# Low parts of the channel MLPs' second weights: a DMA adds the block to its negated high part, in place of a subtraction on VectorE

## The chip, the cores and the metric

One core of one Trainium2 chip. The metric is device time in microseconds: two runs of the kernel before took 1291.55 and 1291.85 us, median 1291.7.

## The reference

Two layers, each a token mixer followed by a channel MLP, on 512 tokens of width 1024. What matters here is the channel MLP, with 4096 hidden features:

```
for i in range(DEPTH):
    ...
    h = rmsnorm(x, norm_g[i, 2]) * (1.0 + sc2) + sh2
    y = jnp.square(jax.nn.relu(h @ ffn_w1[i])) @ ffn_w2[i]
    x = x + g2 * rmsnorm(y, norm_g[i, 3])
```

ffn_w2[i] is 4096 x 1024 in float32. Everything is float32.

## The kernel before

All large products are float32 products made of three products in float32r: each operand is split into a high part, which is its rounding to float32r, and a low part, the difference. mm3 issues high x high, then high x low, then low x high, where the activations are the stationary operand in the second product of the MLP and the weights the moving one.

A channel MLP (ffn) runs in two halves of 2048 hidden features. In a half, the first projection makes 16 tiles of hidden features: TensorE fills a PSUM bank, ScalarE applies relu into a tile t, POOL squares it, ScalarE rounds it to the high part, VectorE subtracts to the low part (tiles a). Then the second product runs over two column blocks of 512 outputs (cb) and two groups of eight K-chunks (k0): w_rows loads four K-chunks by 512 columns as one raw tile of 1 MB, and conv splits it in two blocks [128, 2, 512]; two calls make the four blocks of a group. In a group, four token tiles t follow one another, and each goes through all four blocks: 24 products per token tile, 96 per group, 6 per token tile and block. So there are four groups in a half and 16 such groups in the kernel.

conv makes the high part whi on ScalarE (a cast) and the low part wlo on VectorE (a subtraction). Both come from the pool wp with four buffers each, shared with all other weights; raw tiles come from rp with three buffers, all loads on SP's queue. While the last token tile of a group runs, TensorE releases a block's two buffers after the sixth product on it, and the next group's block is formed into them.

After the first part of the mLSTM mixer the order on each engine is not the order of the code: a scheduler sets it from its own costs (pinned is False from there on), and each engine runs its own list in order. In the lists below a name's last number tells tiles apart.

Of the kernel before, what the change touches and what calls it, by code (L numbers as in the profile page):

```python
# [8 lines left out]
F32 = mybir.dt.float32  # L9
F32R = mybir.dt.float32r  # L10
# [5 lines left out]
P = 128  # L16
# [17 lines left out]
def trunk(ctx: ExitStack, tc: tile.TileContext, x, c, norm_g, ada_w, ada_b, ffn_w1, ffn_w2,  # L34
# [5 lines left out]
    class Engine:  # L40
        """an engine whose instructions keep their traced order while `pinned` is set."""

# [56 lines left out]

# [1 line left out]
    ident = cp.tile([P, P], F32, name="ident")  # L101
# [19 lines left out]

    # silu of the conditioning vector, one column per K-chunk
    ck = cp.tile([8, P], F32, name="ck")
# [8 lines left out]

    # per-feature columns: norm_g (64), hnorm_g (8), b_b_in first half (16); ada_b (96)
    pk = A()[:, 0:2 * P].rearrange("p (a b) -> p a b", a=2)
# [16 lines left out]

# [1 line left out]
    def ada_load(l, vs, vc, k):  # L153
# [37 lines left out]
    def ada_ab(l, vs, vc, ng, k):  # L191
        """scale/shift columns for feature chunk k: h = A * xn + B."""
        raw = ada_load(l, vs, vc, k)
        acc = R().rearrange("p (c i f) -> p c (i f)", c=2, i=2)
        ada_init(raw, acc)
        ada_acc(raw, acc, range(6))
        return ada_fin(ada_tr(acc), l, vs, vc, ng, k)

    def ada_g(box, l, v, ng):
        """gate * norm gain, broadcast over partitions: [P, D]."""  # L200
        g = gp.tile([P, D], F32, tag="g", name=nm("g"))
        box.g = g
        w = ada_w[l].rearrange("(k p) f -> p k f", p=P)
        for s in range(2):
            f0 = v * D + s * S
            acc = R()
            pool.memset(acc, 0.0)
            ld.dma_start(acc[0:1, :], ada_b[l:l + 1, f0:f0 + S])
            for hf in range(2):
                raw = rp.tile([P, 4, S], F32, tag="raw", name=nm("raw"))  # L210
                ld.dma_start(raw, w[:, hf * 4:hf * 4 + 4, f0:f0 + S])
                for j in range(4):
                    kk = hf * 4 + j
                    dve.scalar_tensor_tensor(out=acc, in0=raw[:, j], scalar=cact[:, kk:kk + 1],
                                             in1=acc, op0=ALU.mult, op1=ALU.add)
                yield
            ngb = R()
            ld.dma_start(ngb, norm_g[l, ng:ng + 1, s * S:(s + 1) * S].broadcast_to([P, S]))
            ps = bank3()
            hi, lo = T(F32R), T(F32R)  # L220
            act.copy(hi, acc)
            dve.tensor_sub(lo, acc, f32(hi))
            pe.matmul(ps, lhsT=ones, rhs=hi, start=True, stop=False)
            pe.matmul(ps, lhsT=ones, rhs=lo, start=False, stop=True)
            dve.tensor_mul(g[:, s * S:(s + 1) * S], ps, ngb)
            yield

# [1 line left out]
    def conv(raw_ap, scale=None, lo_eng=None):  # L229
        """exact split of a weight block (optionally with its rows scaled) into two float32r parts."""  # L230
        shp = list(raw_ap.shape)
        hi = wp.tile(shp, F32R, tag="whi", name=nm("whi"))
        lo = wp.tile(shp, F32R, tag="wlo", name=nm("wlo"))
        if scale is None:
            act.copy(hi, raw_ap)
            (lo_eng or dve).tensor_sub(lo, raw_ap, f32(hi))
        else:
            for i, c in enumerate(scale):
                act.activation(hi[:, i], raw_ap[:, i], AF.Copy, scale=c)
                dve.scalar_tensor_tensor(out=lo[:, i], in0=raw_ap[:, i], scalar=c, in1=f32(hi[:, i]),  # L240
                                         op0=ALU.mult, op1=ALU.subtract)
        return hi, lo

    def w_cols(w, f0):
        """two blocks [P, KC, 128] of 128 output features each."""
        raw = rp.tile([P, KC, 2 * P], F32, tag="raw", name=nm("raw"))
        ld.dma_start(raw, w[:, f0:f0 + 2 * P].rearrange("(k p) f -> p k f", p=P))
        return [conv(raw[:, :, i * P:(i + 1) * P]) for i in range(2)]

    def w_rows(w, k0, f0, scale=None):  # L250
        """four K-chunks x 512 output features, as two blocks [P, 2, 512]."""
        raw = rp.tile([P, 4, S], F32, tag="raw", name=nm("raw"))
        ld.dma_start(raw, w[k0 * P:(k0 + 4) * P, f0:f0 + S].rearrange("(k p) f -> p k f", p=P))
        return [conv(raw[:, 2 * i:2 * i + 2], scale and scale[k0 + 2 * i:k0 + 2 * i + 2]) for i in range(2)]
# [5 lines left out]

    # At the end of a sub-layer the first transposes of token tile t are queued behind the product
    # of K-chunk j of a unit u; units 0..3 are the last token tiles, 4.. the next sub-layer's first.
    places = {0: (2, 1), 1: (3, 1), 2: (4, 6), 3: (6, 2)}
    held = {}

    def behind(ins, later):
        """queue ins behind a later traced product."""
        nosync = mybir.DependencyInfo(mybir.DependencyClass.NoSync, mybir.DependencyReason.DATA)
        tc.add_manual_dep(ins.ins, later.ins.name, nosync, reason="issue order")

    class HT:
        """normalised, modulated activations: [feature, token], split."""

# [23 lines left out]

# [1 line left out]
    def rstd_of(parts):  # L299
        """(sum of parts + eps) ** -0.5, parts already hold means."""  # L300
        v = small(1)
        if len(parts) == 2:
            dve.tensor_scalar(v, parts[0], parts[1], EPS, ALU.add, ALU.add)
        else:
            dve.tensor_scalar_add(v, parts[0], EPS)
        r = small(1)
        pool.tensor_tensor(out=r, in0=v, in1=mhalf[:, 0:1], op=ALU.pow)
        return r
# [35 lines left out]
    def residual(t, yg, mss):  # L344
        """x += yg * rstd, yg = gate * norm gain * y in two halves."""
        r = rstd_of(mss)
# [4 lines left out]
    def out_proj(w, h, prep, nk, after, scale=None):  # L351
        """y = h @ w (token major), x += g * rmsnorm(y); after(t) follows each token tile."""
        y = [[None] * 2 for _ in range(NT)]
# [19 lines left out]

# [1 line left out]
    def ffn(l, h, prep, after):  # L375
# [3 lines left out]
        for half in range(2):  # L379
# [37 lines left out]
            for cb in range(2):  # L417
                banks = [bank() for _ in range(NT)]
                for k0 in range(0, 16, 8):
                    blks = w_rows(w2, half * 16 + k0, cb * S) + w_rows(w2, half * 16 + k0 + 4, cb * S)  # L420
                    for t in range(NT):
# [13 lines left out]

# [1 line left out]
    def mlstm(h, prep, after):  # L437
# [3 lines left out]
        for t in range(NT):  # L441
            xx = xp.tile([P, D], F32, tag="x", name=f"x{t}")
            ld.dma_start(xx, x[0, t * P:(t + 1) * P, :])
            xt.append(xx)
        # gate weights, padded with zero columns
        wgs = w.rearrange("(k p) f -> p k f", p=P)
# [107 lines left out]
        qT, kT = [], []  # L554
        # gates: rows 0..7 input gate, 32..39 forget gate
        gt = A()
# [24 lines left out]

        # k
        for f0 in (512, 768):
# [6 lines left out]

        # cumulative log forget gate per chunk, heads on partitions
        ps = bank2()
# [61 lines left out]
        def decay(n):  # L654
            """exp(u_j - m_i), zero for j > i; heads of one parity to a tile."""
            dec.append([])
# [10 lines left out]

        # v, token major with a column of ones per head; three heads to a tile
        vt = [[A(shape=(P, 3, DV + 1)) for _ in range(3)] for _ in range(NT)]
# [31 lines left out]

        # output gate
        so = [[None] * 2 for _ in range(NT)]
# [34 lines left out]
        def mixed(n):  # L738
            ts = slice(n * P, (n + 1) * P)
            pr = dec[n]  # L740
            # columns of the small tiles: e * 4 + p for head 2 * p + e
            ex = scv[:, n, 64:72].rearrange("p (a e) -> p e a", e=2)
# [92 lines left out]

# [1 line left out]
    def sgu(h, prep, after):  # L837
# [8 lines left out]
        def ln_cols():  # L846
            """layer norm gain and bias as feature columns."""
            pk = A()[0:2 * NG, 0:P]
# [6 lines left out]
        def mix_weights(q):  # L855
            """causal spatial weights of four groups, transposed, and their row sums."""
            ws = A()
# [22 lines left out]
        def offsets(q):  # L880
            """what the mix adds to u's factor besides gain * mixed: bias * row sum + bs."""
            rb = A()
# [97 lines left out]

# [1 line left out]
    def store(t):  # L982
# [3 lines left out]
    class Prep:  # L986
        """gate of this sub-layer and scale/shift of the next, in steps run among other work."""

# [63 lines left out]
```

## Time and profile before

| | |
|---|---|
| timed runs, median | 1291.7 us (1291.55 to 1291.85) |
| profiled execution, first to last instruction | 1288.8 us |
| TensorE busy | 1241.9 us |
| VectorE busy | 679.2 us |
| ScalarE busy | 523.9 us |
| POOL busy | 240.0 us |
| read from HBM | 171.11 MB |

The profile is of one execution. The timed runs hold what lies before the first and after the last instruction as well, 2.9 us at the median. PE is TensorE, DVE VectorE, ACT ScalarE, SPq and POOLq the queues of SyncE and GpSimd that issue DMAs. Nearly every instruction carries line 50, that of the helper which records it, so instructions are told apart by the tiles they write and read: wlo<-raw,whi is the subtraction of conv, ps<-wlo,a a product of the second MLP projection with a low part of the weights.

### The profile page before, as it was taken

How to read it: one execution, taken by the hardware profiler on the slowest of the kernel's cores; microseconds unless marked ns; L12 is line 12 of the kernel's file. 1: busy time of each engine (PE TensorE's matmuls, PEld its weight loads, DVE VectorE, ACT ScalarE, POOL GpSimd, SP SyncE). 2: the span in 40 equal slices, each digit the busy share in tenths (PEclk: the TensorE clock that was granted, in tenths of full speed). 3: DMA queues.
4: the chain of work that ended last, by engine and by line, in shares of the span. 5: the costliest groups of instructions: out<-in, count | busy, mean ns of one | idle time of the engine just before them, and what ended most of it. 6: DMA issues, size and time to landing. Idle time of an engine off the chain costs nothing. (4 is left out here: it accounts for less than half of the span.)

```text
span 1288.8 us, 15198 instructions
## 1 busy us (share of the span) xinstructions
PE 1241.9 (96%) x5849; PEld 1019.1 (79%) x5849; DVE 679.2 (53%) x1124; ACT 523.9 (41%) x923; POOL 240.0 (19%) x230
## 2 busy tenths in 40 slices
PE   3999899999999999999999999999999999999997
PEld 2677777888778888888778888888887888888886
DVE  6897666576863343323786766623566222333225
ACT  4535534384433244413563644323653321343221
POOL 5602311013320022200120023200132200122000
PEclk9999999999999999999999999999999999999999
DMA  9756842425762443222367555322255214322201
GB/s 278 225 186 188 256 125 75 137 74 163 214 212 98 132 138 98 98 98 74 130 200 255 158 153 146 109 101 69 95 165 171 98 66 131 99 98 98 98 33 66
DMA packets 165610, 174.25 MB, mean 135 GB/s; under 512 B 6168, under 2 KB 120936, under 8 KB 165536
## 3 DMA queue, kind: packets, MB, share of 16 engines
q1 hardware_dynamic: 165408, 173.17, 42.5%
q8 instruction: 46, 0.75, 0.2%
q14 instruction: 28, 0.23, 0.1%
q0 software_dynamic: 128, 0.09, 0.0%
HBM read 171.11 MB, written 2.14 MB: 134 GB/s over the span
## 5 line engine op out<-in xcount | busy, mean ns | idle before, releaser
L50 PE MATMUL ps<-whi,a 128*128 128x512 f32 x1408 | 437.1, 390 | 0.0
L50 DVE TENSOR_TENSOR wlo<-raw,whi 128x1024 fp32r<-128x1024 f32 x196 | 241.4, 1236 | 313.8 <-ACT whi L50 304.0
L50 ACT CAST whi<-raw 128x1024 fp32r<-128x1024 f32 x196 | 205.0, 1050 | 287.0 <-PE ps L50 252.1
L50 PEld LDWEIGHTS ps<-whi,a 128*128 128x128 f32 x1408 | 264.3, 188 | 54.5
L50 PE MATMUL ps<-hlo,whi 128*128 128x512 f32 (+1 forms) x744 | 277.3, 373 | 2.9 <-POOL hlo L50 2.9
L50 PE MATMUL ps<-hhi,whi 128*128 128x512 f32 (+1 forms) x744 | 279.1, 375 | 0.5 <-ACT whi L50 0.5
L50 PE MATMUL ps<-hhi,wlo 128*128 128x512 f32 (+1 forms) x744 | 277.2, 373 | 0.7 <-DVE wlo L50 0.7
L50 PE MATMUL ps<-wlo,a 128*128 128x512 f32 x704 | 274.4, 390 | 1.0 <-DVE wlo L50 1.0
L50 PEld LDWEIGHTS ps<-hlo,whi 128*128 128x128 f32 x744 | 140.3, 189 | 28.3 <-POOL hlo L50 4.2
L50 DVE SCALAR_TENSOR_TENSOR r<-raw,cact,r 128x256 f32<-128x256 f32 (+1 forms) x256 | 149.3, 622 | 23.8 <-ACT r L50 16.6
L50 PEld LDWEIGHTS ps<-hhi,wlo 128*128 128x128 f32 x744 | 140.2, 188 | 25.6 <-DVE wlo L50 1.5
L50 PEld LDWEIGHTS ps<-hhi,whi 128*128 128x128 f32 x744 | 140.3, 189 | 24.4 <-ACT whi L50 0.9
L50 POOL TENSOR_TENSOR t<-t 128x512 f32<-128x512 f32 x64 | 98.4, 1537 | 314.9 <-ACT t L50 314.9
L50 PEld LDWEIGHTS ps<-wlo,a 128*128 128x128 f32 x704 | 132.2, 188 | 28.9 <-DVE wlo L50 1.9
L50 POOL TENSOR_TENSOR s<-s,mhalf 128x1 f32<-128x1 f32 (+1 forms) x40 | 33.9, 847 | 378.8 <-DVE s L50 371.4
L50 PE MATMUL ps<-whi,hhi 128*128 128x512 f32 x256 | 101.6, 398 | 1.4 <-ACT whi L50 1.3
L50 PE MATMUL ps<-wlo,hhi 128*128 128x512 f32 x256 | 100.5, 393 | 2.4 <-DVE wlo L50 2.4
L50 PE MATMUL ps<-whi,hlo 128*128 128x512 f32 x256 | 100.2, 392 | 0.0
L50 DVE TENSOR_TENSOR a<-t,a 128x512 fp32r<-128x512 f32 x64 | 44.3, 692 | 77.2 <-ACT a L50 75.8
L50 ACT CAST a<-t 128x512 fp32r<-128x512 f32 x64 | 39.7, 621 | 103.3 <-POOL t L50 103.3
L50 POOL TENSOR_TENSOR r<-r 128x256 f32<-128x256 f32 x32 | 32.9, 1028 | 185.4 <-DVE r L50 159.4
L50 PEld LDWEIGHTS ps<-wlo,hhi 128*128 128x128 f32 x256 | 48.1, 188 | 14.4 <-DVE wlo L50 5.1
(128 smaller groups left out, 996.7 us busy)
## 6 DMA issues: line engine op xcount, KB each, us to landing
raw<-in_ffn_w SPq DMA_DIRECT2D x64, 1024.0 KB, 5.3
raw<-in_ada_w SPq DMA_DIRECT2D x64, 512.0 KB, 5.6
raw<-in_ada_w SPq DMA_DIRECT2D x16, 1024.0 KB, 5.0
raw<-in_b_w_in SPq DMA_DIRECT2D x16, 1024.0 KB, 5.5
raw<-in_a_w_in SPq DMA_DIRECT2D x10, 1024.0 KB, 5.1
raw<-in_b_w_out SPq DMA_DIRECT2D x8, 1024.0 KB, 6.3
raw<-in_a_w_out SPq DMA_DIRECT2D x4, 1024.0 KB, 5.0
x<-in_x SPq DMA_DIRECT2D x4, 512.0 KB, 7.6
```

Of the source, the lines that this page charges most:

```text
L50: r = f(*a, **k)
```

## The change

In the second product of the channel MLPs w_rows_acc stands in place of w_rows. ScalarE writes the negated block, rounded to float32r, into lo; a DMA issued by POOL reads the same block from HBM a second time and adds it onto lo; ScalarE casts the block to hi as before. VectorE has no part in it. The other weights keep conv. Lines that only drop a comment are left out.

```diff
@@ -242,13 +242,29 @@
+    def w_rows_acc(w, k0, f0):
+
+
+        raw = rp.tile([P, 4, S], F32, tag="raw", name=nm("raw"))
+        src = w[k0 * P:(k0 + 4) * P, f0:f0 + S].rearrange("(k p) f -> p k f", p=P)
+        ld.dma_start(raw, src)
+        out = []
+        for i in range(2):
+            hi = wp.tile([P, 2, S], F32R, tag="whi", name=nm("whi"))
+            lo = wp.tile([P, 2, S], F32R, tag="wlo", name=nm("wlo"))
+            act.activation(lo, raw[:, 2 * i:2 * i + 2], AF.Copy, scale=-1.0)
+            pool.dma_start(lo, src[:, 2 * i:2 * i + 2], accum_op=ALU.add)
+            act.copy(hi, raw[:, 2 * i:2 * i + 2])
+            out.append((hi, lo))
+        return out
+
@@ -417,7 +433,7 @@
-                    blks = w_rows(w2, half * 16 + k0, cb * S) + w_rows(w2, half * 16 + k0 + 4, cb * S)
+                    blks = w_rows_acc(w2, half * 16 + k0, cb * S) + w_rows_acc(w2, half * 16 + k0 + 4, cb * S)
```

The scheduler orders the engines anew around it. On TensorE, the start of the fourth group of the first half in layer 0; a is a tile of hidden features, ps the bank of a token tile (3694 is the first). Before:

```order
L50 MATMUL ps_3694<-whi_3816,a_3044 128x512
L50 MATMUL ps_3694<-wlo_3817,a_3044 128x512
L50 MATMUL ps_3694<-whi_3816,a_3045 128x512
L50 MATMUL ps_3694<-whi_3816,a_3082 128x512
L50 MATMUL ps_3694<-wlo_3817,a_3082 128x512
L50 MATMUL ps_3694<-whi_3816,a_3083 128x512
L50 MATMUL ps_3694<-whi_3820,a_3134 128x512
L50 MATMUL ps_3694<-wlo_3821,a_3134 128x512
```

The same place now, where 3702 is the bank of the first token tile and 3703 that of the second:

```order
L50 MATMUL ps_3702<-whi_3828,a_3044 128x512
L50 MATMUL ps_3703<-whi_3828,a_3044 128x512
L50 MATMUL ps_3702<-wlo_3829,a_3044 128x512
L50 MATMUL ps_3702<-whi_3828,a_3045 128x512
L50 MATMUL ps_3702<-whi_3828,a_3082 128x512
L50 MATMUL ps_3702<-wlo_3829,a_3082 128x512
L50 MATMUL ps_3702<-whi_3828,a_3083 128x512
L50 MATMUL ps_3702<-whi_3833,a_3134 128x512
L50 MATMUL ps_3703<-wlo_3829,a_3044 128x512
L50 MATMUL ps_3703<-whi_3828,a_3045 128x512
L50 MATMUL ps_3702<-wlo_3834,a_3134 128x512
```

Products of the second token tile now stand ahead of the first product with each low part. The first use of the four low parts, counted from that of the first, was 0, 6, 12 and 18 products and is now 0, 8, 17 and 25 (up to 28 in some groups).

On ScalarE, the four blocks of that same group. Before:

```order
L50 CAST whi_3816<-raw_3814 128x1024
L50 CAST whi_3820<-raw_3814 128x1024
L50 CAST whi_3826<-raw_3824 128x1024
L50 CAST whi_3830<-raw_3824 128x1024
L50 ACTIVATE r_3983<-raw_3980,cact 128x256 x2
```

And now, a negation ahead of each cast:

```order
L50 ACTIVATE wlo_3829<-raw_3826 128x1024
L50 CAST whi_3828<-raw_3826 128x1024
L50 ACTIVATE wlo_3834<-raw_3826 128x1024
L50 CAST whi_3833<-raw_3826 128x1024
L50 ACTIVATE wlo_3841<-raw_3838 128x1024
L50 CAST whi_3840<-raw_3838 128x1024
L50 ACTIVATE wlo_3846<-raw_3838 128x1024
L50 CAST whi_3845<-raw_3838 128x1024
```

Each block takes two passes on ScalarE, the negation first.

On POOL, the end of the first projection and the first group of the second product, where t are the squares of hidden features and r partial sums of the adaLN weights. Before:

```order
L50 TENSOR_TENSOR r_3377<-r_3377 128x256
L50 TENSOR_TENSOR r_3431<-r_3431 128x256
L50 TENSOR_TENSOR t_3367<-t_3367 128x512
L50 TENSOR_TENSOR t_3421<-t_3421 128x512
L50 TENSOR_TENSOR r_3983<-r_3983 128x256
```

And now:

```order
L50 TENSOR_TENSOR r_3431<-r_3431 128x256
L50 DMA wlo_3457<-in_ffn_w 128x2x512
L50 DMA wlo_3462<-in_ffn_w 128x2x512
L50 TENSOR_TENSOR t_3367<-t_3367 128x512
L50 DMA wlo_3469<-in_ffn_w 128x2x512
L50 TENSOR_TENSOR t_3421<-t_3421 128x512
L50 DMA wlo_3474<-in_ffn_w 128x2x512
L50 DMA wlo_3577<-in_ffn_w 128x2x512
```

The adding DMAs of the first group stand between the last squares; those of the groups after it follow one another.

## Rows read from the trace of the kernel before

**Rows 1.** The page, parts 1 and 2: busy time, and the span in 40 slices.

```profile
span 1288.8 us, 15198 instructions
...
PE 1241.9 (96%) x5849; PEld 1019.1 (79%) x5849; DVE 679.2 (53%) x1124; ACT 523.9 (41%) x923; POOL 240.0 (19%) x230
...
PE   3999899999999999999999999999999999999997
...
PEclk9999999999999999999999999999999999999999
```

**Rows 2.** The chain that ended last, in order of time: start, us, what.

```profile
990.16 285.63 PE ps L50 x1260
```

**Rows 3.** Windows of the four second products: length, busy time by engine, clock, DMA share, GB/s.

```profile
core 0: us, PE busy (x) PEld busy (x) DVE busy (x) ACT busy (x) POOL busy (x), PEclk, DMA share, GB/s
371.50:458.40 86.90, 86.22 (x380) 71.04 (x379) 26.75 (x36) 23.52 (x30) 2.51 (x3) 1.00 0.37 118
...
sum 346.90, PE 345.94 PEld 285.47 DVE 109.57 ACT 91.23 POOL 13.73; mean PE 86.48 PEld 71.37 DVE 27.39 ACT 22.81 POOL 3.43
```

**Rows 4.** Waits of PE over the span: us in total, times, longest.

```profile
PE ps L50 <- DVE wlo L50: 4.1, 8, 1.1
```

**Rows 5.** Timeline of ACT, then DVE, where one group passes to the next: start, us.

```profile
410.82 1.05 ACT L50 CAST whi<-raw 128x1024 fp32r<-128x1024 f32 x1 [0.77 <-PE ps L50]
412.18 1.06 ACT L50 CAST whi<-raw 128x1024 fp32r<-128x1024 f32 x1 [0.31 <-PE ps L50]
413.54 1.06 ACT L50 CAST whi<-raw 128x1024 fp32r<-128x1024 f32 x1 [0.30 <-PE ps L50]
414.90 0.59 ACT L50 COPY a<-ps 128x512 f32<-128x512 f32 x1 [0.30 <-PE ps L50]
415.39 1.05 ACT L50 CAST whi<-raw 128x1024 fp32r<-128x1024 f32 x1
432.58 1.05 ACT L50 CAST whi<-raw 128x1024 fp32r<-128x1024 f32 x1 [16.14 <-PE ps L50]
...
411.91 3.95 DVE L50 TENSOR_TENSOR wlo<-raw,whi 128x1024 fp32r<-128x1024 f32 x3 [16.45 <-ACT whi L50]
```

**Rows 6.** Groups by form: count, busy us, mean ns, idle before.

```profile
L50 DVE TENSOR_TENSOR wlo<-raw,whi 128x1024 fp32r<-128x1024 f32 x196 | 241.4, 1236 | 313.8 <-ACT whi L50 304.0 <-PE pt L50 2.9 <-PE ps L50 0.3
...
L50 ACT CAST whi<-raw 128x1024 fp32r<-128x1024 f32 x196 | 205.0, 1050 | 287.0 <-PE ps L50 252.1 <-issue 30.7 <-DMA raw<-in_ffn_w 3.4
```

**Rows 7.** DMAs that POOL issued: queue; issues, KB, us to landing; one on POOL's timeline.

```profile
q0 software_dynamic: 128, 0.09, 0.0%
...
a<-in_ada_b POOLq DMA_DIRECT2D x1, 48.0 KB, 5.5
a<-in_norm_g POOLq DMA_DIRECT2D x1, 32.0 KB, 5.8
...
a<-in_a_hnorm_g POOLq DMA_DIRECT2D x1, 4.0 KB, 5.2
a<-in_b_b_in POOLq DMA_DIRECT2D x1, 8.0 KB, 5.4
...
4.83 0.55 POOL L50 DMA_DIRECT2D a<-in_ada_b  x1
```

**Rows 8.** DMA in 410 to 434 us, slices of 0.6 us; then issues in 370 to 460.

```profile
GB/s 0 27 0 0 0 0 0 0 0 89 154 362 410 399 387 172 256 387 387 382 109 0 0 0 0 0 0 0 0 0 0 0 0 0 0 0 0 0 0 0
...
raw<-in_ffn_w SPq DMA_DIRECT2D x8, 1024.0 KB, 5.1
```

**Rows 9.** Timelines of ACT and POOL at the first group of a stretch.

```profile
372.40 0.59 ACT L50 ACTIVATE t<-ps 128x512 f32<-128x512 f32 x1
...
389.06 1.05 ACT L50 CAST whi<-raw 128x1024 fp32r<-128x1024 f32 x1 [14.30 <-PE ps L50]
...
373.07 1.04 POOL L50 TENSOR_TENSOR t<-t 128x512 f32<-128x512 f32 x1 [3.12 <-ACT t L50]
```

## The prediction

> **What bounds the kernel now.** I read the page first. TensorE is busy for 1241.9 of 1288.8 us, and its granted clock is at the upper level (2.4 GHz) in every slice, also in the first, where TensorE works only three tenths of the time [rows 1]. So there is no clock term: waits of some microseconds have not lowered the clock in this trace. The chain of work shows TensorE's real pace: 1260 products in 285.63 us, 0.2267 us each [rows 2]; the mean durations of about 0.39 us on the page overlap and are not a pace.
>
> Then the stretches that the change touches: the products with the second weights, two halves in each of two layers. The four windows last 346.9 us together and TensorE is busy for 345.94 of them [rows 3]. They run at TensorE's pace, with about 1 us idle in all. Over the whole span products wait for a low part for 4.1 us, in 8 waits [rows 4]. That is all a faster low part could give back, and most of it belongs to other weights.
>
> Each stretch has four groups of 96 products (four weight blocks, four token tiles), 21.76 us long: first casts at 410.82 and 432.58 us [rows 5]. So there are 16 groups: 4 open a stretch, 12 follow another group. Only four buffers exist for each part, so a following group's blocks can only be formed while the last token tile of the previous group runs. In [rows 5] ACT's casts start at 410.82, 412.18, 413.54 and, after a copy, 415.39, the first three as TensorE releases the buffers, 1.36 us apart; VectorE's subtractions follow at once, and the first low part is there at about 413.15 (411.91 + 1.24). It is wanted at about 415.1: 18 products of 0.2267 us after the release the next group opens, at 414.90, and its second product reads it. The margin is about 2 us. This margin is what the change spends.
>
> **What is removed.** 64 subtractions of 1.236 us, 79 us of VectorE [rows 6]. VectorE is busy 109.57 us of these 346.9 us [rows 3] and is not what TensorE waits for, so this is worth the 1 us of idle time at most.
>
> **What is added on ScalarE.** 64 negations. The same engine makes the high part of the same block in 1.050 us [rows 6]; I take 1.05 each, 67 us. ScalarE goes from 91 to about 158 of 346.9 us, so its sum fits. But negation and cast now alternate on one queue: a block takes 2.1 us of ScalarE where buffers come free every 1.36 us. The four negations end at 411.87, 413.97, 416.07 and 418.17 us, if the first starts at 410.82, and the last at 418.76 where the copy of 0.59 us stands among them [rows 5].
>
> **What is added on the DMA side.** 64 transfers of 512 KB, each issued by POOL after its negation, which the low part now waits for. POOL is busy 13.7 us in the stretches [rows 3], and issuing takes 0.55 us on it [rows 7]. Behind a waiting issue stand only the next issues, except in a group that opens a stretch: there the squares of the last hidden features stand between the issues, as the order shows. They feed the group after it, so a late issue there has a whole group as cover. The loads on SP are unchanged; a raw buffer is now free after ScalarE's last pass instead of VectorE's, within a microsecond or two, and a load has most of a 21.76 us group to arrive.
>
> **What TensorE allows.** The new order has moved the first use of each low part back. In a following group the first low part is the third product, and the others follow 8, 17 and 25 products later. With the group opening at 414.90 they are wanted at 415.35, 417.17, 419.21 and 421.02 us. From the negation's end that leaves 3.5, 3.2, 3.1 and 2.9 us (2.3 with the copy) for issue, transfer and completion. TensorE's queue is in order, so a late low part stops everything behind it.
>
> **What the transfer takes.** The trace of before has no adding DMA, so I bound it from two sides. The low side is a plain load from SP: 1024 KB land 5.1 us after the issue, and while moving they go at 360 to 410 GB/s [rows 8], some 2.7 us of data, so 2.4 us are fixed. For 512 KB that is 2.4 + 1.35 = 3.75 us. The high side is the software queue: the four transfers that POOL issued carry 4 to 48 KB and land after 5.2 to 5.8 us [rows 7], almost all of it fixed, though other transfers were running. An add must also read the old contents of the tile, so the bytes read double, 2.7 us: 5.5 + 2.7 = 8.2 us. I take a fixed part midway, 4.0 us, since the queue is the software one but less crowded here, and two reads: 6.7 us.
>
> These transfers also stand in each other's way. They are issued 2.1 us apart and each occupies the engines for 2.7, so the fourth is pushed by 3 x 0.6 = 1.8 us. The load of 1 MB for a coming group, 2.7 us of data, starts when the first raw buffer is free, near 415; I let half of it, 1.3, fall ahead of the fourth block. So the fourth low part lands at 418.17 + 6.7 + 1.8 + 1.3 = 428.0 and is wanted at 421.0: 7.0 us late. (The first alone would be 3.2 late; the waits of one group overlap, so the largest counts.)
>
> In a group that opens a stretch three of the four buffers come free earlier, during the first projection. Only the fourth is late: ScalarE's relu of the last feature starts at 372.40, the negation behind it ends near 374.0, and POOL's square runs to 374.11 [rows 9], so the issue is near 374.1 and the landing 380.8. The group opens at about 371.4 (a group ahead of 393.1, itself 18 products after the cast at 389.06 [rows 9]); the fourth low part is product 26 or 27 there, 377.1: 3.7 us late.
>
> Sum: 12 x 7.0 + 4 x 3.7 = 99 us, less the 1 us of idle time. 1288.8 + 98 = 1386.8 us. The runs' median of 1291.7 us lies 2.9 above the span of the profiled execution, so 1390 us. By the low side (3.75 us, no queueing but half a load ahead of the fourth, 0.7) a following group loses 418.17 + 3.75 + 0.7 - 421.0 = 1.6 us and an opening one about 0.8: 22 us, 1313. By the high side with a whole load ahead, 9.9 and 5.2: 139 us, 1430.
>
> **The Trainium skill on the transfer.** Rows show 5.2 to 5.8 us for tiny transfers of the software queue [rows 7]. DMA: Bandwidth & Descriptors, section Anatomy of one DMA, gives a fit for that queue of about 2.0 us plus the bytes at 436 GB/s. As an estimate from that page 512 KB would take 3.2 us, and the change would just be hidden. The four rows speak against its fixed part. Collectives: The Full Stack, under the bandwidth ceiling, says that an adding step runs at about half the rate of a copy because it reads two sources; as an estimate from both pages that is 4.4 us, some 2 to 4 us late per group and about 1335 us. No row of before shows an add.
>
> **Rivals.** *Hidden, not slower.* The low part lands within the 2.9 to 3.5 us that TensorE allows, and the transfers do not queue. For it speaks that the reordered products leave room and that the DMA engines are idle after each load [rows 8]. The fit of DMA: Bandwidth & Descriptors in the Trainium skill would bring it about. Against it speak all four POOL rows [rows 7], and that even half a megabyte by the fastest load needs 3.75. It would give 1288.8 - 1 + 2.9 = 1291 us, at best 1287 if all waits of [rows 4] went too. It decides at the allowance; up to 1.6 us late per group the loss stays within 2% (16 x 1.6 = 26 us). Chance 0.12.
>
> *A slow add.* The engines may add at half the rate again, 5.4 us per transfer. Then the landing takes 4.0 + 5.4 = 9.4, and the fourth is pushed by 3 x 3.3 = 9.9: 418.17 + 9.4 + 9.9 + 1.3 - 421.0 = 17.8 us per following group, 6.4 in an opening one, 239 us, 1530 us. Nothing in the trace bounds the rate of an add from above, which is why I keep it. Chance 0.27.
>
> *Forecast.* Transfers at the copy rate with two reads, late in every group: 1313 to 1430 us, likeliest 1390. Chance 0.59. A gain of over 2% would need 26 us and I find 5 at most; 0.02 is left.
>
> **Range and chances.** The range runs from 1296, which takes in a change nearly hidden, to 1560, past the middle of the slow add. About 2% is what a measurement of this kernel can tell from no change. Faster 0.02, within 2% 0.13 (hidden, and the lowest end of the forecast), slower 0.85.
>
> **What will show it.** In the profile after: matmuls of these stretches waiting for DMA on wlo, about once per group and up to 7 us; the four windows grown from 346.9 to about 445 us, with TensorE's busy sum there near 346; the adding transfers landing after 6 to 9 us with issues some 2.1 us apart; VectorE down by 79 us and ScalarE up by 67; the clock unchanged. I am wrong if the waits stay under a microsecond, if one wait per group is far over 10 us, or if the loss stands outside these stretches.

## The result

The changed kernel takes 1449.39 us (1448.81 to 1449.97) against 1291.7 before: ratio 1.1217, interval 1.1197 to 1.1238. That is 157.7 us slower, where 98 were forecast. The profiled execution spans 1448.2 us, 159.4 more than before.

The page of the changed kernel, lines that answer to [rows 1], [rows 6] and [rows 7]:

```profile
span 1448.2 us, 15333 instructions
...
PE 1296.0 (89%) x5849; PEld 1041.5 (72%) x5849; DVE 600.4 (41%) x1060; ACT 580.8 (40%) x987; POOL 310.1 (21%) x294
...
PEclk9999999999989999999899999999999999999998
...
q0 software_dynamic: 17536, 33.65, 13.5%
...
L50 POOL DMA_DIRECT2D wlo<-in_ffn_w x64 | 77.7, 1221 | 323.0 <-ACT wlo L50 317.5
...
L50 ACT ACTIVATE wlo<-raw 128x1024 fp32r<-128x1024 f32 x64 | 67.4, 1053 | 184.5 <-PE ps L50 182.8
...
wlo<-in_ffn_w POOLq DMA_DIRECT2D x64, 512.0 KB, 10.4
```

VectorE is down by 78.8 us and ScalarE's negations add 67.4, as worked out. An adding transfer lands 10.4 us after its issue at the median, and the clock has dips inside the span that it had not before.

The windows of the four second products, which answer to [rows 3]:

```profile
373.50:502.00 128.50, 101.01 (x388) 77.11 (x386) 9.40 (x21) 35.43 (x43) 18.24 (x17) 0.89 0.64 146
589.40:717.00 127.60, 100.83 (x383) 77.09 (x382) 18.14 (x31) 37.11 (x55) 20.24 (x18) 0.89 0.54 125
1106.70:1233.20 126.50, 99.62 (x386) 77.22 (x386) 3.31 (x4) 33.31 (x38) 16.68 (x14) 0.91 0.52 116
1320.10:1439.70 119.60, 99.33 (x385) 77.51 (x383) 14.87 (x24) 30.95 (x42) 18.32 (x17) 0.91 0.49 107
sum 502.20, PE 400.78 PEld 308.93 DVE 45.73 ACT 136.79 POOL 73.48; mean PE 100.20 PEld 77.23 DVE 11.43 ACT 34.20 POOL 18.37
```

They grew from 346.9 to 502.2 us, 155.3 of the 159.4. The loss is where it was placed. TensorE's waits over the whole span, beside [rows 4]:

```profile
PE ps L50 <- DMA wlo<-in_ffn_w: 100.6, 46, 5.5
...
PE ps L50 <- DVE wlo L50: 3.7, 7, 1.1
```

These 100.6 us look like the 99 of the forecast, and the rest like slow products: 502.2 less 100.6 less 1536 products of 0.2267 us leaves about 53 us, at a granted clock of 0.89 to 0.91. That reading is wrong, as one group shows. Three timelines show the second following group of the first stretch, beside [rows 5] (a row is the start, the duration, the engine and the work; in brackets the idle time ahead of it and what ended it). ScalarE's, the first negation of this group and of the next:

```profile
435.02 1.06 ACT L50 ACTIVATE wlo<-raw 128x1024 fp32r<-128x1024 f32 x1 [0.55 <-PE ps L50]
...
467.05 1.06 ACT L50 ACTIVATE wlo<-raw 128x1024 fp32r<-128x1024 f32 x1 [23.88 <-PE ps L50]
```

POOL's, the four issues of the adds:

```profile
436.38 1.20 POOL L50 DMA_DIRECT2D wlo<-in_ffn_w  x1 [26.25 <-ACT wlo L50]
438.27 1.20 POOL L50 DMA_DIRECT2D wlo<-in_ffn_w  x1 [0.69 <-ACT wlo L50]
440.17 1.20 POOL L50 DMA_DIRECT2D wlo<-in_ffn_w  x1 [0.69 <-ACT wlo L50]
442.54 1.20 POOL L50 DMA_DIRECT2D wlo<-in_ffn_w  x1 [1.17 <-DMA wlo<-in_ffn_w]
```

TensorE's, the products that a landing released:

```profile
442.42 0.50 PE L50 MATMUL ps<-wlo,a 128*128 128x512 f32 x1 [2.69 <-DMA wlo<-in_ffn_w]
448.91 0.50 PE L50 MATMUL ps<-wlo,a 128*128 128x512 f32 x1 [3.11 <-DMA wlo<-in_ffn_w]
...
455.80 0.50 PE L50 MATMUL ps<-wlo,a 128*128 128x512 f32 x1 [0.52 <-DMA wlo<-in_ffn_w]
```

The first negation starts at 435.02, the fourth low part lands at 455.8, 20.8 us later, and the next group's first negation starts at 467.05, 11.25 us after that. The group is 32.0 us long, not 21.76. The two loads for the coming group are issued at 438.94 and 443.20, ahead of the second landing. The windows of the same group:

```profile
439.00:442.40 3.40, 0.74 (x4) 0.28 (x2) 0.00 (x0) 3.40 (x5) 1.68 (x2) 1.00 1.00 201
442.40:448.90 6.50, 3.37 (x8) 2.14 (x8) 0.00 (x0) 0.77 (x1) 1.20 (x1) 0.74 1.06 254
448.90:455.80 6.90, 6.37 (x20) 4.42 (x20) 0.00 (x0) 0.00 (x0) 0.00 (x0) 0.75 1.08 250
455.80:467.00 11.20, 11.20 (x49) 9.26 (x50) 0.00 (x0) 0.00 (x0) 0.00 (x0) 1.00 0.02 7
```

From 439.0 to 455.8 the DMA share is 1.00 to 1.08: the DMA engines are busy throughout, with the four adds and these two loads. In this group the clock is low only while landings are awaited. After the fourth landing TensorE runs 49 products in 11.20 us at full clock, 0.2286 each. Between landings a slow product only fills time in which TensorE would have waited: it makes the wait look shorter, and costs nothing. So the length of a following group is the time from its first negation to the fourth landing, plus some 50 products at full pace. Over the 12 following groups the first part is 20.5 us at the mean (15.5 to 22.3), and what slow clock costs after the fourth landing is 0.1 us a group.

### The profile page after: what moved, and what is told of

It is laid out like the page before. It is cut to its first block, busy times and chain, and to the rows that moved or that the text cites. A ratio compares the mean times of both kernels' runs of the same rounds, so it can differ in the third digit from the quotient of the medians.

```text
span 1448.2 us, 15333 instructions
## 1 busy us (share of the span) xinstructions
PE 1296.0 (89%) x5849; PEld 1041.5 (72%) x5849; DVE 600.4 (41%) x1060; ACT 580.8 (40%) x987; POOL 310.1 (21%) x294
## 3 DMA queue, kind: packets, MB, share of 16 engines
q0 software_dynamic: 17536, 33.65, 13.5%
## 4 chain that ended last, share of the span: by engine, by line
PE 47%; issue 17%; DMA 15%; DVE 9%; POOL 6%; ACT 6%; SPq 1%; POOLq 0%; DVEq 0%; ACTq 0%
PE ps L50 44%; DMA wlo<-in_ffn_w 8%; DMA raw<-in_ada_w 4%; DVE a L50 3%; DVE r L50 3%; POOL wlo L50 2%; PE pt L50 2%; DVE wlo L50 2%; POOL t L50 2%; ACT whi L50 1%; POOL s L50 1%; ACT wlo L50 1%; ACT t L50 1%; SPq L50 1%; ACT j L50 1%
## 5 line engine op out<-in xcount | busy, mean ns | idle before, releaser
L50 PE MATMUL ps<-whi,a 128*128 128x512 f32 x1408 | 462.4, 411 | 0.0
L50 PE MATMUL ps<-wlo,a 128*128 128x512 f32 x704 | 296.8, 422 | 101.0 <-DMA wlo<-in_ffn_w 100.6
L50 PEld LDWEIGHTS ps<-whi,a 128*128 128x128 f32 x1408 | 282.2, 200 | 59.1
L50 DVE TENSOR_TENSOR wlo<-raw,whi 128x1024 fp32r<-128x1024 f32 x132 | 165.3, 1259 | 233.5 <-ACT whi L50 229.0
L50 PEld LDWEIGHTS ps<-wlo,a 128*128 128x128 f32 x704 | 141.1, 200 | 155.3 <-DMA wlo<-in_ffn_w 126.4
L50 POOL DMA_DIRECT2D wlo<-in_ffn_w x64 | 77.7, 1221 | 323.0 <-ACT wlo L50 317.5
L50 POOL TENSOR_TENSOR t<-t 128x512 f32<-128x512 f32 x64 | 90.0, 1406 | 254.0 <-ACT t L50 254.0
L50 ACT ACTIVATE wlo<-raw 128x1024 fp32r<-128x1024 f32 x64 | 67.4, 1053 | 184.5 <-PE ps L50 182.8
L50 DVE TENSOR_TENSOR a<-a,ps 128x512 f32<-128x512 f32 x24 | 16.3, 683 | 192.8 <-PE ps L50 192.8
## 6 DMA issues: line engine op xcount, KB each, us to landing
wlo<-in_ffn_w POOLq DMA_DIRECT2D x64, 512.0 KB, 10.4
```

The costliest lines, as they stand in the source:

```text
L50: r = f(*a, **k)
```

## Experiments

The ratios below are to runs of the kernel before that were timed beside each experiment. Their median is 1293.07 us for VectorE's addition, the copy, the adds with low parts last and the threefold subtraction, and 1292.09 us for the other four.

**Who delays: ScalarE's second pass, or the DMA?** VectorE adds in place of the DMA.

```diff
-            pool.dma_start(lo, src[:, 2 * i:2 * i + 2], accum_op=ALU.add)
+            dve.tensor_add(lo, raw[:, 2 * i:2 * i + 2], f32(lo))
```

> As the changed kernel, with the negation on ScalarE kept, but VectorE adds the block to it in place of the DMA. Theory (the products wait for the adding DMA, and what they lose besides is clock after those waits): 1288 to 1300 us, products wait for wlo under 10 us in all, granted clock 1.00 in the stretches. Rival (the second pass on ScalarE delays the high and the low parts): over 1340 us, with waits for ACT whi or DVE wlo in every group.

Measured: 1293.1 us, ratio 0.9998 (0.9988 to 1.0008). The 64 negations are there (ScalarE 580.3 us busy) and cost nothing; TensorE waits 2.7 us in all for low parts by VectorE. The second pass is not the cause.

**Is it the transfer's time, or a fixed part of POOL's queue?** The same DMA without the add.

```diff
-            pool.dma_start(lo, src[:, 2 * i:2 * i + 2], accum_op=ALU.add)
+            pool.dma_start(lo, src[:, 2 * i:2 * i + 2])
```

> As the changed kernel, but POOL's DMA writes the block over the negated part and does not add, so the low part used is the block itself; all waits and the issue are kept. Theory (the transfer's time on the DMA engines counts, and an add costs two reads): packets of 2 KB take about 90 ns in place of 190, the landing falls from a median of 10.4 us to 6 to 8, waits from 100 us to 30 to 60, total 1335 to 1385 us. Rival (the fixed part of the software queue counts, whatever the DMA does): landing still over 9 us, total over 1420 us.

Measured: 1391.86 us, ratio 1.0761 (1.0737 to 1.0785). The page of the copying kernel, its queue and the landing of its copies:

```profile
q0 software_dynamic: 17536, 33.65, 8.4%
...
wlo<-in_ffn_w POOLq DMA_DIRECT2D x64, 512.0 KB, 7.1
```

And TensorE's waits for the copies, in its view of waits:

```profile
PE ps L50 <- DMA wlo<-in_ffn_w: 66.1, 40, 5.0
```

As many packets and bytes take 8.4% of 16 engines' span of 1392.4 us, where the add took 13.5% of 1448.2. Divided by 64 transfers that is 1.83 us of all engines for a copy and 3.05 for an add: an add costs 1.67 times a copy. By row of 2 KB that is 114 and 191 ns on one engine, where some 90 and 190 were expected. The landing falls to 7.1 us, as the theory said, and first negation to fourth landing to 16.2 us. The total is 7 us above the range given and the waits 6 us above theirs. The shortest copy of this run landed after 3.9 us and half of them after more than 7.1, so a large part of the landing is neither the add nor a fixed part; two runs below look for it.

**Can the landing be hidden?** Products with high parts first, those with low parts last; the cast ahead of the negation; in the last group of each layer the kernel before.

```diff
+    def proj_late(banks, blks, h, k0, first, last):
+        for t in range(NT):
+            for j in range(8):
+                wh = blks[j // 2][0]
+                hh, hl = h(k0 + j, slice(t * P, (t + 1) * P))
+                pe.matmul(banks[t], lhsT=hh, rhs=wh[:, j % 2], start=first and j == 0, stop=False)
+                pe.matmul(banks[t], lhsT=hl, rhs=wh[:, j % 2], start=False, stop=False)
+        for b in range(4):
+            for t in range(NT):
+                for j in (2 * b, 2 * b + 1):
+                    hh, _ = h(k0 + j, slice(t * P, (t + 1) * P))
+                    pe.matmul(banks[t], lhsT=hh, rhs=blks[b][1][:, j % 2], start=False,
+                              stop=last and j == 7)
...
+            act.copy(hi, raw[:, 2 * i:2 * i + 2])
             act.activation(lo, raw[:, 2 * i:2 * i + 2], AF.Copy, scale=-1.0)
             pool.dma_start(lo, src[:, 2 * i:2 * i + 2], accum_op=ALU.add)
-            act.copy(hi, raw[:, 2 * i:2 * i + 2])
...
-                    blks = w_rows_acc(w2, half * 16 + k0, cb * S) + w_rows_acc(w2, half * 16 + k0 + 4, cb * S)
+                    end = half == 1 and cb == 1 and k0 == 8
+                    rows = w_rows if end else w_rows_acc
+                    blks = rows(w2, half * 16 + k0, cb * S) + rows(w2, half * 16 + k0 + 4, cb * S)
+                    if not end:
+                        proj_late(banks, blks, z, k0, k0 == 0, k0 == 8)
```

> As the changed kernel, but in 14 of the 16 groups all 64 products with high parts of the weights go first, and the 32 with low parts last, block by block; the cast comes ahead of the negation. The last group of each layer's second half keeps the order by token tile and VectorE's subtraction. The first low part is then wanted some 14.5 us after the group opens instead of 0.5, the fourth some 20. Theory (landing against first use): the adds are hidden, waits for wlo under 15 us, clock 0.99 to 1.00, 1289 to 1310 us, with the transfers landing as late as now. Rivals (ScalarE's passes, or the traffic itself, slow TensorE): over 1340 us.

Measured: 1294.59 us, ratio 1.0009 (1.0000 to 1.0018). Its page, the granted clock and the adds:

```profile
PEclk9999999999999999999999999999999999999999
...
wlo<-in_ffn_w POOLq DMA_DIRECT2D x56, 512.0 KB, 10.5
```

56 adds land as late as in the changed kernel, nothing waits for them (no wait for wlo from a DMA is left in the view of waits) and the clock is full in the stretches. The loads, 56 of the 64 adds and as many negations are there. What is changed is the order, and with it the distance from landing to first use, and the subtraction in two groups; of the 12.2% about 0.1% is left.

The same order without any adding DMA, with VectorE's subtraction throughout:

```diff
-                    rows = w_rows if end else w_rows_acc
+                    rows = w_rows
```

> The order of products of the run with low parts last, with every low part by VectorE's subtraction and no adding DMA. If the order itself costs and gives nothing, the same time as before within 0.3%, 1289 to 1297 us; if the order alone were what brought the adding kernel back, this one would lie below the kernel before by over 0.5%.

Measured: 1293.55 us, ratio 1.0010 (1.0001 to 1.0020). The order alone gives nothing. Neither version lies below the kernel before.

**Who lowers the clock?** First the subtraction on VectorE again, as in the kernel before, but done three times; the diff is against the changed kernel.

```diff
-            act.activation(lo, raw[:, 2 * i:2 * i + 2], AF.Copy, scale=-1.0)
-            pool.dma_start(lo, src[:, 2 * i:2 * i + 2], accum_op=ALU.add)
             act.copy(hi, raw[:, 2 * i:2 * i + 2])
+            for _ in range(3):
+                dve.tensor_sub(lo, raw[:, 2 * i:2 * i + 2], f32(hi))
```

> The kernel before, with VectorE's subtraction of these blocks done three times over, so a low part takes 3.7 us of VectorE and no DMA is added. The fourth low part of a group is then 5 to 7 us late. Theory (the clock falls where TensorE has waited): waits of 60 to 90 us for DVE wlo, mean granted clock below 0.99, and 20 to 50 us more for products at the lower level: 1370 to 1430 us. Rival (the adding DMAs themselves, by traffic or power, lower the clock): waits the same, clock 1.00, 1350 to 1385 us.

Measured: 1320.48 us, ratio 1.021 (1.0189 to 1.0230), only 20.0 us of waits for low parts. The expectation was wrong about the waits, so this run says little on the clock. The scheduler knows what a subtraction costs: it moved the first use of the fourth low part to 41 products after that of the first, where it had put 25 to 28 for the DMA. One group's subtractions in VectorE's timeline:

```profile
418.61 13.96 DVE L50 TENSOR_TENSOR wlo<-raw,whi 128x1024 fp32r<-128x1024 f32 x12 [9.08 <-ACT whi L50]
```

And the one wait that they leave, in TensorE's:

```profile
423.42 0.50 PE L50 MATMUL ps<-wlo,a 128*128 128x512 f32 x1 [0.99 <-DVE wlo L50]
```

14 us of work on the low parts leave 1.0 us of waiting. Then six times:

```diff
-            for _ in range(3):
+            for _ in range(6):
```

> The kernel before, with VectorE's subtraction of these blocks done six times over (7.4 us a block, 29.6 us for the four of a group that TensorE needs 21.8 us for), and no added DMA. It should lose some 8 us in each of 12 groups, 95 to 125 us in all. Theory (waits of some microseconds, close together, let TensorE's clock fall, whoever causes them): half-rate stretches in most groups, as in the changed kernel, and since a slow product only fills time in which TensorE would wait, little is lost on top: 1385 to 1425 us. Rival (the clock falls because of the DMAs' traffic): waits as large and no half-rate stretches.

Measured: 1407.79 us, ratio 1.0895 (1.0874 to 1.0917). The windows of its four stretches, in sum:

```profile
sum 458.90, PE 384.45 PEld 303.05 DVE 439.99 ACT 86.35 POOL 7.29; mean PE 96.11 PEld 75.76 DVE 110.00 ACT 21.59 POOL 1.82
```

A shorter window within the first stretch:

```profile
432.00:434.50 2.50, 2.50 (x7) 1.94 (x6) 2.50 (x3) 0.48 (x1) 0.00 (x0) 0.50 0.76 197
```

What stands just before it, a window and the product that ends the wait:

```profile
428.00:431.00 3.00, 1.06 (x5) 0.56 (x3) 3.00 (x4) 1.65 (x2) 0.00 (x0) 1.00 0.00 0
...
431.49 0.79 PE L50 MATMUL ps<-wlo,a 128*128 128x512 f32 x1 [2.43 <-DVE wlo L50]
```

And its view of waits:

```profile
PE ps L50 <- DVE wlo L50: 67.2, 34, 7.0
```

VectorE is busy for 440 of 459 us and sets the time; the clock has half-rate pieces here too (0.50 in the window shown), with no adding DMA, and here after a wait of 2.43 us in which the DMA engines were idle for most of the time (share 0.00 in the window before). So the lower clock comes with the waits and needs no add; and the run above with adds and no waits has none in the stretches.

**What delays the landing?** First the add reads the raw tile, so a raw tile is held until its adds have landed.

```diff
-            pool.dma_start(lo, src[:, 2 * i:2 * i + 2], accum_op=ALU.add)
+            pool.dma_start(lo, raw[:, 2 * i:2 * i + 2], accum_op=ALU.add)
```

> As the changed kernel, but the adding DMA reads the block from its raw tile in SBUF and not from HBM again. A raw tile is then held until its two adds have landed, so the load that takes its place cannot share the DMA engines with them; only one of the two loads still falls among the four adds. Theory (adds and loads share the DMA engines, and a group's length is the time from its first negation to the fourth landing plus about 11.5 us of products): first negation to fourth landing 17 to 19 us in place of 21, total 1400 to 1430 us. Rival (an add's time is set by its own fixed part or by HBM reads): no change, 1440 to 1455 us, or with HBM as the limit landings under 15 us and under 1385 us.

Measured: 1367.03 us, ratio 1.058 (1.0559 to 1.0601); first negation to fourth landing 15.4 us at the mean of the following groups. Queue and landing:

```profile
q0 software_dynamic: 9344, 33.65, 13.7%
...
wlo<-raw POOLq DMA_DIRECT2D x64, 512.0 KB, 5.6
```

The direction is the theory's, the size is not: 33 us below the low end. The adds take about as much of the engines (13.7% of 1365.7 us, 2.92 us for one), so an add without the read from HBM is not much cheaper there. TensorE's waits for them in the following groups are at most 1.7 us long, and the clock stayed at 1.00 there. But a transfer is now rows of 4 KB in place of 2 KB, half as many packets, issued in 0.87 us in place of 1.20, and the first add lands 5.9 us after its negation starts, against 7.4, ahead of any load; and in the group looked at the load issued at 404.50 moved its bytes only from 409 on, when the adds were nearly done. Which of these brought the rest, and why that load held back, stays open. Then the loads are taken away instead:

```diff
-        raw = rp.tile([P, 4, S], F32, tag="raw", name=nm("raw"))
         src = w[k0 * P:(k0 + 4) * P, f0:f0 + S].rearrange("(k p) f -> p k f", p=P)
-        ld.dma_start(raw, src)
+        if k0 % 16 == 0 and f0 == 0:
+            one = rp.tile([P, 4, S], F32, tag="raw", name=nm("raw"))
+            ld.dma_start(one, src)
+            kept[0] = one
+        raw = kept[0]
```

> As the changed kernel, but each half loads one raw tile of the second weights only, and all negations and casts of the half read that tile, so seven of eight loads are left out and nothing competes with the adds (which still read their own blocks from HBM). Theory (both loads of a coming group fall among the adds and push the fourth landing): first negation to fourth landing 15 to 16 us, as in the last group of the changed kernel, which has no such loads behind it, in place of 21; 12 groups shorter by 5 us or more, total 1365 to 1395 us. Rival (the adds alone fill the time): landing and total unchanged, over 1430 us.

Measured: 1384.93 us, ratio 1.0719 (1.0697 to 1.0740). One following group, from its first negation, in the timeline:

```profile
423.15 1.06 ACT L50 ACTIVATE wlo<-raw 128x1024 fp32r<-128x1024 f32 x1 [0.54 <-PE ps L50]
...
430.80 0.50 PE L50 MATMUL ps<-wlo,a 128*128 128x512 f32 x1 [2.93 <-DMA wlo<-in_ffn_w]
433.31 0.50 PE L50 MATMUL ps<-wlo,a 128*128 128x512 f32 x1 [0.41 <-DMA wlo<-in_ffn_w]
435.86 0.50 PE L50 MATMUL ps<-wlo,a 128*128 128x512 f32 x1 [0.21 <-DMA wlo<-in_ffn_w]
438.82 0.50 PE L50 MATMUL ps<-wlo,a 128*128 128x512 f32 x1 [0.40 <-DMA wlo<-in_ffn_w]
```

Queue and landing on its page:

```profile
q0 software_dynamic: 17536, 33.65, 14.3%
...
wlo<-in_ffn_w POOLq DMA_DIRECT2D x64, 512.0 KB, 6.8
```

The first add lands 7.65 us after its negation starts, as in the changed kernel (442.42 - 435.02 = 7.4). The next three follow after 2.5, 2.55 and 2.96 us, where the changed kernel has 6.5 to the second and 6.9 for the two after it. The fourth is there after 15.7 us in place of 20.8 (means of the following groups 16.3 and 20.5). The engines' time for an add is the same, 14.3% of 1382.1 us by 64 or 3.09 us. So the loads for the coming group, 2 MB by both raw tiles, share the engines with the adds and push the later landings.

## Why the forecast was right in sign and too small

- *Nothing to gain on VectorE, nothing to pay on ScalarE*: right. The first run shows the second, 1293.1 us with the negations kept. The runs with low parts last show the first: VectorE is busy for 609.0 us with the adds and 676.8 with the subtractions, at ratios of 1.0009 and 1.0010.
- *The margin*: right. The low parts are wanted some 3 us after the negations and land far later, in every group; late products alone bring the time back (1294.59).
- *The transfer alone*: right in sum. 6.7 us from negation end to landing were taken; 442.42 less 436.08 is 6.3. 2.7 us of engine time were taken for two reads; 3.05 were measured, which leaves some 3.2 for the rest in place of 4.0. The 4.0 lay midway between two bounds, so part of the agreement is luck. The Trainium skill's fit (DMA: Bandwidth & Descriptors, Anatomy of one DMA) gives 3.2 us for 512 KB; no add from HBM landed in under 5.6 us. Its rule on adds (Collectives: The Full Stack, the bandwidth ceiling: half the rate, for two source reads), stated there for a step of a collective, comes near, with 1.67 times a copy's time.
- *Queueing of the four adds among themselves*: about right. Without loads the fourth came 15.7 us after the first negation in the group shown and 16.3 at the mean; by the terms of the forecast without its load it would have been 15.9 (1.05 + 6.7 + 6.3 + 1.8).
- *"I let half of it, 1.3, fall ahead of the fourth block"*: this is the term that was mis-sized. Both loads of 1 MB, not half of one, fall among the adds; leaving them out gave 4.2 us a following group at the mean and 5.1 in the groups set side by side above, where 1.3 was forecast. The fourth landing came 20.5 us after the first negation in place of 17.2, so a following group is 10.3 us late and not 7.0: 124 of the 159.4 us.
- *An opening group*: 3.7 us were forecast. In the second stretch, which opens at 589.4, the next negation starts at 613.48, 24.1 us later, where 78 products of 0.2267 us would put it 17.7 later: 6.4 us. The landing is 7.85 us after its issue and not 6.7, and here the clock does cost something, since 52 products after the landing take 13.5 us and not 11.8. Counted the same way, the other three lose 10.7, 6.0 and 6.2 us; in the first stretch, with 10.7, the adds land 8.3 to 13.9 us after their issue and TensorE waits for all four, not for the fourth alone. The four opening groups together come to 29 us.
- *No clock term*: the reason was wrong, the sum hardly. The prediction read from [rows 1] that waits had left the clock of the kernel before at its upper level, also in the first slice. That reading does not hold. The trace has no record of the clock ahead of 28.1 us, and the page counts time without a record as full. TensorE's own timeline of the kernel before shows the pace there, behind waits of 3.07 and 5.42 us:

```profile
26.59 0.63 PE L50 MATMUL ps<-hlo,whi 128*128 128x512 f32 x1
27.01 0.63 PE L50 MATMUL ps<-hhi,wlo 128*128 128x512 f32 x1
27.44 0.63 PE L50 MATMUL ps<-hhi,a 128*128 128x512 f32 x1
27.87 0.51 PE L50 MATMUL ps<-hlo,a 128*128 128x512 f32 x1
...
28.68 0.40 PE L50 MATMUL ps<-hlo,a 128*128 128x512 f32 x1
28.91 0.62 PE L50 MATMUL ps<-hhi,a 128*128 128x512 f32 x2
29.37 0.40 PE L50 MATMUL ps<-hlo,a 128*128 128x512 f32 x1
```

Products follow one another after 0.42 to 0.43 us up to 27.87 and after 0.23 from 28.68 on: the lower level, 1.2 GHz, and then the upper. In the stretches of the changed kernel the clock fell to the lower level around waits of 2.1 to 5.5 us, single ones too; but nearly all of it fell where TensorE waited for landings, 0.1 us a following group and up to 1.7 an opening one are left. That the missing term cost the forecast so little is luck: the slow products happened to lie between landings.

- The rivals: *hidden* is out as the kernel stands, and true once the order makes room. *A slow add* is out by the 3.05 us, although the total went in its direction.
- The range: 1449.39 lies above the forecast's own 1313 to 1430 and below the slow add's 1530. The range up to 1560 holds it only because it was widened for the slow add, which did not happen. That is luck, and not the mechanism.
- The signs: the loss stands in the stretches, VectorE and ScalarE moved as said. Not as said were the windows (502.2 us for 445), TensorE's busy sum in them (400.8 for 346, slow products included), the waits (46 in 16 groups for one a group, the longest 5.5), the landing (10.4 us for 6 to 9) and the clock.

## What to carry to other kernels

Put a DMA into a chain that had 2 us of margin only after finding work to place between its landing and its first use; here 64 of 96 products could go first and hid 10 us of landing, though without a gain over the kernel before. Count every transfer that is set free at the same moment: the passes on ScalarE that opened the way for the adds also freed the raw tiles, and with them the loads that shared the engines. When waits and a lower clock stand in the same window, do not add them: measure from the last landing to the next release, and see how many products ran there at what pace.

## What was not expected of the hardware

- POOL's issue of an add takes 1.20 us for 256 rows of 2 KB and 0.87 for 128 rows of 4 KB, a plain copy of 256 rows 0.72, against 0.55 for the small ones of [rows 7].
- An add from SBUF and one from HBM take nearly the same time of the DMA engines (13.7% of 1365.7 us and 14.3% of 1382.1, by 64: 2.92 and 3.09 us).
- The granted clock fell to 0.50 with DMAs as with VectorE as the cause of the waits, and one wait was enough. In the second stretch of the changed kernel, the product that ends a wait and the window from there:

```profile
600.03 0.80 PE L50 MATMUL ps<-wlo,a 128*128 128x512 f32 x1 [4.15 <-DMA wlo<-in_ffn_w]
...
600.00:603.30 3.30, 3.27 (x8) 2.60 (x9) 0.00 (x0) 0.00 (x0) 0.00 (x0) 0.50 0.00 0
```
